# A three-block network on one core: the state-space stage re-paced and its products halved by columns, wider products after two norms

## The chip, the cores and the metric

The kernel runs on one core of a Trainium2 chip. The metric is the device time of the program in microseconds (us), lower is better; a kernel is run several times and the median counts.

## What is computed

One sequence of 512 tokens of width 2048 goes through three layers, in float32. The first is a state-space (S5) layer:

```python
xn = rmsnorm(h, g_pre)
u, z = jnp.split(xn @ w_in, 2, axis=-1)
y = s5_ssm(u, a_re, a_im, log_dt, b_re, b_im, c_re, c_im, d_skip)
y = jax.nn.gelu(y)
y = y * jax.nn.sigmoid(y @ w_glu + b_glu)
y = y * jax.nn.silu(z)
return h + rmsnorm(y @ w_out, g_post)
```

`s5_ssm` runs a complex recurrence of 64 states over the 512 steps in each of 128 groups of 16 channels, plus `d_skip * u`. The second layer is causal attention with forget gates, whose keys, values and gates come from a projection (`shared_kv`) of the first layer's normed output. The third mixes a windowed attention with an RWKV recurrence, after one wide product `h @ w_in_2`, and ends in a product and a norm.

## The kernel before

Activations lie transposed, 16 pages of 128 channels by 512 tokens. A product of float32 accuracy is made of three matmuls: each operand is split into a rounded part and a rest (`hi`, `lo` of the activations by `split`, L165 ff.; `wh`, `wl` of the weights by `wnext`, L188 ff., ScalarE making the first and VectorE the second), and `gemm` (L214) runs hi*wh, lo*wh, hi*wl over 16 k, 48 matmuls of 128x512 per output tile, in four chunks of weights. Weights come by DMA from ScalarE's queue, three chunks ahead.

The stages are `phase1` (32 tiles of `w_in` with the S5 work between them), `phase2` (the gate: 16 tiles, then `out_norm` with 16 tiles of `w_out`, the norm, the residual sum and the next layer's normed activations), `phase4` (value slabs, then 16 key tiles), `phase5` and `phase6` (attention, `out_norm` again), `phase7` and `phase8` (third layer).

In `phase1` the tiles 0 to 15 of `order1` hold u, the rest z; from the sixth tile on a u tile comes every 1.35 tiles. For each u tile j (8 groups) the S5 work is put into a list of due times by `later`, counted in chunks of weights, and `tick` calls what is due: `s5_pool` (GpSimd builds the tables In and Ox for two half-tiles hb), `s5_mats` (kb, the products that make a Toeplitz block, sent by 8 small DMAs of Kt into toep; tb, transposes of In, copied to InT), `s5_phase` (rotation factors Ec, Es), `s5_x` (xb = InT*U, rotation, scan Gs, rotation back to H) and `s5_y` (yb = toep*U + Ox*H, gelu to q, 8 DMAs to y2d). u goes out to memory and comes back as U, regrouped. The S5 matmuls are plain float32 with 64 moving columns (kb and tb 128); a float32 matmul leaves two records in the trace.

The final order of instructions on each engine is made by a scheduler at build time, from the order of these calls and its own model of durations. Each engine runs its instructions strictly in that order. SyncE's queue issues the S5 DMAs and the loads. The pool `tp` of 8 buffers (`tmp`) is shared by everything that is short-lived.

`out_norm` (L743) sums squares, forms the scale (`rstd`, L277), multiplies it into the 16 pages (VectorE for k < 3, GpSimd for the others, L761 and L763), adds the residual (L766 with a permuted token order after the S5 layer, L769 without after attention) and splits. The next products then take the pages k by k: `phase4` with `slab` (L229; four outputs of 272 columns), `phase7` with `gemm`.

```python
self.later(0, self.s5_pool, 2 * j)
self.later(2, self.s5_pool, 2 * j + 1)
self.later(6, self.s5_mats, 2 * j)
self.later(8, self.s5_mats, 2 * j + 1)
...
self.later(10, self.s5_x, j)
self.later(14, self.s5_y, j)
```

Of the kernel before, what the change touches and what calls it, by code (L numbers as in the profile page):

```python
# [42 lines left out]
def lay(inp):  # L43
# [3 lines left out]
    o["xT"] = np.ascontiguousarray(x.reshape(NCK, T, D).transpose(2, 1, 0).reshape(D, S))  # L47
    o["w1"] = _tiles(a["s5_w_in"][0])
# [91 lines left out]
    dd = np.zeros((16, G, 16), np.float32)  # L140
    for c in range(16):
        dd[c, :, c] = a["s5_d"][0].reshape(G, 16)[:, c]
    o["s5dd"] = np.ascontiguousarray(dd.reshape(16, 32, 64).transpose(1, 0, 2))
# [5 lines left out]
class Kern:  # L149
# [80 lines left out]
    def slab(self, act, outs, W, kc=2):  # L230

        nc = self.nc
        for c in range(KT // kc):
# [229 lines left out]

    def s5_pool(self, hb):
# [19 lines left out]
        self.In[hb] = prod("In", Q, B1, B2, 8, 2)  # L484
        self.Ox[hb] = prod("Ox", PT, C1, C2, 9, 5)
        self.dd[hb] = sp.tile([16, 64], F32, tag="dd", name="dd", bufs=4)
        nc.sync.dma_start(self.dd[hb], self.I["s5dd"][hb])

    def s5_mats(self, hb):

        nc, sp = self.nc, self.sp
        In, Ox = self.In.pop(hb), self.Ox[hb]
        kb = self.bank("kb")
        for g in range(4):
            nc.tensor.matmul(kb[:16, g * 128:(g + 1) * 128], In[:, g, 7, :],
                             Ox[:, g, 0:8, :].rearrange("p k c -> p (k c)"), start=True, stop=True)
        tb = self.bank("tb")
        for g in range(4):
            nc.tensor.transpose(tb[:, g * 128:(g + 1) * 128], In[:, g].rearrange("p s c -> p (s c)"), self.ident)
        Kt = sp.tile([16, 4, 128], F32, tag="Kt", name="Kt", bufs=2)  # L500
        k3 = kb[:16].rearrange("p (g k) -> p g k", k=128)
        nc.scalar.activation(Kt[:, :, 16:], k3[:, :, 16:], AF.Copy)

        nc.vector.tensor_tensor(Kt[:, :, :16], k3[:, :, :16], self.dd.pop(hb).rearrange("p (g c) -> p g c", c=16), ALU.add)
        Tp = self.toep[hb % len(self.toep)]
        for s in range(8):
            nc.sync.dma_start(Tp[s * 16:(s + 1) * 16, :, s * 16:128], Kt[:, :, 0:(8 - s) * 16])
        InT = sp.tile([128, 4, 128], F32, tag="InT", name="InT", bufs=3)
        nc.scalar.activation(InT.rearrange("p g k -> p (g k)"), tb, AF.Copy)
        self.InT[hb] = InT  # L510
# [13 lines left out]
    def s5_phase(self, m):  # L524
# [5 lines left out]
        Cc = sp.tile(shp, F32, tag="Cc", name="Cc", bufs=1)  # L530
        Ss = sp.tile(shp, F32, tag="Ss", name="Ss", bufs=1)
# [21 lines left out]
    def s5_x(self, j):  # L553

        nc, sp, v = self.nc, self.sp, self.nc.vector
        U = self.U[j]
# [6 lines left out]
        X = sp.tile([128, 512], F32, tag="X", name="X", bufs=1)  # L563
# [5 lines left out]
        Gs = sp.tile([128, 512], F32, tag="Gs", name="Gs", bufs=1)  # L569
        v.tensor_tensor_scan(Gs, rt.rearrange("p g k -> p (g k)"), X, 0.0, ALU.mult, ALU.add)  # L570
        H = sp.tile([128, 8, 64], F32, tag="X", name="H", bufs=1)
        Hf = H.rearrange("p g k -> p (g k)")
        v.tensor_tensor(Hf, Gs, Ec, ALU.mult)
        v.tensor_tensor(m[0:64], Gs[64:128], Es[64:128], ALU.mult)
        v.tensor_tensor(m[64:128], Gs[0:64], Es[0:64], ALU.mult)
        v.tensor_add(Hf, Hf, m)  # L576
        self.H[j] = H

    def s5_y(self, j):
# [3 lines left out]
        for g in range(8):  # L583
            hb = 2 * j + g // 4
            nc.tensor.matmul(yb[:, g * 64:(g + 1) * 64], self.toep[hb % len(self.toep)][:, g % 4, :], U[:, g, :],
                             start=True, stop=False)
            nc.tensor.matmul(yb[:, g * 64 + 1:(g + 1) * 64],  # L587
                             self.Ox[hb][:, g % 4, 1:9, :].rearrange("p k c -> p (k c)"),
                             H[:, g, 0:63], start=False, stop=True)

        ys = self.tmp("ys")
        nc.scalar.activation(ys, yb, AF.Copy)
        q = self.tmp("q")
        nc.scalar.activation(q, ys, AF.Square)
        v = nc.vector
        v.scalar_tensor_tensor(q, q, 1 / 0.044715, ys, ALU.add, ALU.mult)
        nc.scalar.activation(q, q, AF.Tanh, scale=0.7978845608028654 * 0.044715)
        v.scalar_tensor_tensor(q, q, 1.0, ys, ALU.add, ALU.mult)
# [5 lines left out]
    def run(self):  # L604
        tc, nc, I = self.tc, self.nc, self.I
        v = nc.vector
        with ExitStack() as ex:
# [26 lines left out]
            self.wplan(I["wv0"], [0], 544)  # L634
            self.wplan(I["wv"], range(7))
# [22 lines left out]
    def phase1(self):  # L658
        tc, nc, I, v = self.tc, self.nc, self.I, self.nc.vector
        with ExitStack() as ex:  # L660
# [13 lines left out]
            self.toep = [self.bp.tile([128, 4, 128], F32, name=f"toep{i}") for i in range(4)]  # L674
# [12 lines left out]
            self.sp = None  # L687
            for n in self.order1:
                if n < 16:
                    j = n  # L690
                    if self.sp is None:
                        while self.todo:
                            self.tick()
                        b0.__exit__(None, None, None)
                        self.sp = P(name="sp", bufs=2)
                    self.later(0, self.s5_pool, 2 * j)
                    self.later(2, self.s5_pool, 2 * j + 1)
                    self.later(6, self.s5_mats, 2 * j)
                    self.later(8, self.s5_mats, 2 * j + 1)
# [980 lines left out]
```

## Time and profile before

| | |
|---|---|
| median of 3 runs (lowest, highest) | 3218.8 us (3217.1, 3230.14) |
| the profiled execution | 3217.31 us, span 3215.2 us |
| mean granted TensorE clock | 0.966 of full |
| busy: PE, VectorE, ScalarE, GpSimd | 95%, 58%, 35%, 23% of the span |
| S5 stage, from 118 to 566 us | PE busy 424.41 of 448 us, clock 0.93 |

The span runs from the first to the last instruction of the profiled execution, and 2.1 us of its time lie outside. PE is TensorE. The granted clock is given as a share of full speed, so 0.50 is 1.2 GHz and 1.00 is 2.4 GHz. Matmuls are pipelined: one of 128x512 lasts 0.39 us in the trace, but the next starts 0.23 us after it at full clock, so the distance between starts is what it costs.

### The profile page before, as it was taken

What the parts mean: (1) busy time and instruction counts of PE and PEld (TensorE: products, weight loads), DVE (VectorE), ACT (ScalarE), POOL (GpSimd) and SP (SyncE); (2) the same over time, 40 slices, a digit from 0 to 9 for tenths busy, and PEclk for the clock granted to TensorE, in tenths of its full rate; (3) what the DMA queues carried; (4) which work ended last, traced back from release to release, by engine and by line L of the source; (5) the groups of instructions that cost most, each with busy time, mean ns of one, the idle gap of its engine ahead of it and who ended that gap; (6) DMA issues with size and microseconds to landing.
All of it is one profiled execution on the core that took longest, in us unless ns stands there. A gap on an engine that the chain in (4) does not pass through costs nothing. (4 is left out here: it accounts for less than half of the span.)

```text
span 3215.2 us, 44670 instructions
## 1 busy us (share of the span) xinstructions
PE 3046.9 (95%) x16228; PEld 2511.4 (78%) x16228; DVE 1874.8 (58%) x3171; ACT 1129.8 (35%) x2046; POOL 735.9 (23%) x693
## 2 busy tenths in 40 slices
PE   8899999899989999999999997999889999999897
PEld 6777878688869988888888885777679788777685
DVE  9777676443348333555555337488599566645733
ACT  5243343433323222433333334233222344533322
POOL 0656564110020000000000002233378321122200
PEclk9899999899989999999999998999999999999898
DMA  5344444543343333433333336345742433398533
GB/s 155 109 104 108 110 110 111 186 140 111 95 139 122 109 95 95 125 85 86 89 88 84 92 96 185 108 141 174 180 126 93 122 99 99 108 253 216 159 118 108
DMA packets 347837, 396.29 MB, mean 123 GB/s; under 512 B 138416, under 2 KB 184752, under 8 KB 347616
## 3 DMA queue, kind: packets, MB, share of 16 engines
q10 hardware_dynamic: 131328, 237.43, 26.5%
q1 hardware_dynamic: 216288, 156.00, 16.5%
q8 instruction: 128, 2.10, 0.3%
q14 instruction: 93, 0.76, 0.1%
HBM read 324.59 MB, written 59.80 MB: 120 GB/s over the span
## 5 line engine op out<-in xcount | busy, mean ns | idle before, releaser
L225 PE MATMUL acc<-hi,wh 128*128 128x512 f32 x3232 | 1290.7, 400 | 33.5 <-ACT hi L173 14.6
L226 PE MATMUL acc<-lo,wh 128*128 128x512 f32 x3232 | 1287.2, 399 | 14.6 <-DVE lo L177 11.6
L227 PE MATMUL acc<-hi,wl 128*128 128x512 f32 x3232 | 1287.6, 399 | 10.8 <-DVE wl L199 10.6
L199 DVE TENSOR_TENSOR wl<-raw,wh 128x512 fp32r<-128x512 f32 (+1 forms) x912 | 690.9, 760 | 870.4 <-ACT wh L198 850.2
L198 ACT ACTIVATE wh<-raw 128x512 fp32r<-128x512 f32 (+1 forms) x912 | 571.8, 629 | 1428.3 <-PE acc L226 938.4
L225 PEld LDWEIGHTS acc<-hi,wh 128*128 128x128 f32 x3232 | 617.1, 191 | 176.1 <-ACT hi L173 16.1
L226 PEld LDWEIGHTS acc<-lo,wh 128*128 128x128 f32 x3232 | 616.7, 191 | 164.0 <-DVE lo L177 18.9
L227 PEld LDWEIGHTS acc<-hi,wl 128*128 128x128 f32 x3232 | 616.0, 191 | 152.7 <-DVE wl L199 15.4
L244 PE MATMUL vb<-wh,hi 128*128 128x256 f32 (+2 forms) x768 | 218.8, 288 | 7.6 <-ACT hi L176 5.0
L246 PE MATMUL vb<-wh,lo 128*128 128x256 f32 (+2 forms) x768 | 213.5, 288 | 9.3 <-DVE lo L177 9.2
L245 PE MATMUL vb<-wl,hi 128*128 128x256 f32 (+2 forms) x768 | 219.7, 288 | 1.1 <-DVE wl L199 1.0
L857 POOL TENSOR_TENSOR bm<-bias,cmask 128x512 f32<-128x512 f32 x16 | 21.2, 1326 | 691.5 <-DMA bias<-cumd 458.4
L244 PEld LDWEIGHTS vb<-wh,hi 128*128 128x128 f32 x768 | 147.9, 193 | 8.8 <-ACT hi L176 5.2
L246 PEld LDWEIGHTS vb<-wh,lo 128*128 128x128 f32 x768 | 144.5, 192 | 11.6 <-DVE lo L177 11.3
L245 PEld LDWEIGHTS vb<-wl,hi 128*128 128x128 f32 x768 | 148.2, 193 | 2.8 <-DVE wl L199 2.2
L763 POOL TENSOR_TENSOR y<-y,rstd 128x512 f32<-128x512 f32 x26 | 43.8, 1723 | 411.2 <-ACT rstd L295 411.2
L479 POOL TENSOR_TENSOR In<-Q,bc 128x512 f32<-128x512 f32 x32 | 45.7, 1428 | 251.8 <-DMA bc<-in_s5bc 246.4
L1124 POOL TENSOR_TENSOR wg<-Yi 128x3 f32<-128x3 f32 (+56 forms) x114 | 62.6, 549 | 22.1 <-DVE Yi L1125 14.4
L1125 POOL TENSOR_TENSOR Yi<-Yi,wg 128x3 f32<-128x3 f32 (+56 forms) x114 | 62.7, 550 | 8.6
L587 PE MATMUL yb<-H,Ox 128*128 128x63 f32 x256 | 54.6, 299 | 8.4 <-DVE H L576 8.4
L737 POOL TENSOR_TENSOR ld<-ld 128x512 f32<-128x512 f32 x16 | 20.9, 1308 | 179.2 <-DMA ld<-zd 178.5
L1125 DVE TENSOR_TENSOR Yi<-Yi,w 128x504 f32<-128x504 f32 (+29 forms) x99 | 57.5, 604 | 7.5 <-POOL Yi L1125 7.0
(433 smaller groups left out, 3395.6 us busy)
## 6 DMA issues: line engine op xcount, KB each, us to landing
raw<-in_w ACTq DMA_DIRECT2D x744, 256.0 KB
raw<-in_wk ACTq DMA_DIRECT2D x64, 256.0 KB
raw<-in_wv ACTq DMA_DIRECT2D x56, 256.0 KB
ld<-hd SPq DMA_DIRECT2D x48, 256.0 KB
ld<-y2d SPq DMA_DIRECT2D x32, 256.0 KB
hd<-h SPq DMA_DIRECT2D x32, 256.0 KB
Xd<-X SPq DMA_DIRECT2D x32, 256.0 KB
raw<-in_wd ACTq DMA_DIRECT2D x24, 256.0 KB
```

What stands on the lines that cost most here:

```text
L198: nc.scalar.activation(wh, raw, AF.Copy)
L199: nc.vector.tensor_sub(wl, raw, wh.bitcast(F32))
L225: nc.tensor.matmul(acc, wh[:, sl], hi, start=(kk == 0), stop=False)
L226: nc.tensor.matmul(acc, wh[:, sl], lo, start=False, stop=False)
L227: nc.tensor.matmul(acc, wl[:, sl], hi, start=False, stop=(kk == KT - 1))
L244: nc.tensor.matmul(outs[t], hi[:, tk], wh[:, sl], **st)
L245: nc.tensor.matmul(outs[t], hi[:, tk], wl[:, sl], start=False, stop=False)
L246: nc.tensor.matmul(outs[t], lo[:, tk], wh[:, sl], start=False, stop=(kk == KT - 1 and (W > 256 or t % 2 == 1)))
L479: e.tensor_tensor(o, tr, X1.unsqueeze(2).broadcast_to(shp), ALU.mult)
L587: nc.tensor.matmul(yb[:, g * 64 + 1:(g + 1) * 64], self.Ox[hb][:, g % 4, 1:9, :].rearrange("p k c -> p (k c)"), H[:, g, 0:63], start=False ...
L1124: e.tensor_tensor(w, Y[:, a:a + k, t:t + 1].broadcast_to(shp), Y[:, t:t + 1, t + 1:].broadcast_to(shp), ALU.mult)
L1125: e.tensor_tensor(Y[:, a:a + k, t + 1:], Y[:, a:a + k, t + 1:], w, ALU.add)
```

## The change

The S5 calls are no longer tied to the u tiles: they are all entered at the fifth tile, evenly spaced by 1.35 tiles, with the tables of a tile begun one tile earlier than before. `s5_mats` handles a whole tile at once: kb of four groups goes to four column strips of the array (partitions 0, 32, 64, 96 of one bank), the d_skip diagonal is added by small matmuls with the identity, and eight ScalarE copies take the strips to Kt. xb and yb are computed in column halves (`HALF`), two matmuls of 64 output rows where there was one of 128. gelu reads yb in PSUM, without the copy ys. The second rotation multiplies a copy Gw of the scan with swapped halves, made by ScalarE. X, Gs, Gw, Kt, Cc and Ss come from the shared pool of 8 buffers.

After the S5 layer the permuted write moves from `out_norm` to the gate stage, so that the residual is read from x in natural order (`xn`). In `phase4` the first two value slabs advance together, k pair by k pair, and `phase7` begins with four tiles at once (`gemm4`).

```diff
+    def gemm4(self, act):
+        nc = self.nc
+        accs = [self.pq.tile([128, 512], F32, tag="g", name="acc") for _ in range(4)]
+        ws = []
+        for _ in accs:
+            self.tick()
+            ws.append(self.wnext())
+        for k in range(4):
+            hi, lo = act[k]
+            sl = slice(k * 128, k * 128 + 128)
+            for acc, (wh, wl) in zip(accs, ws):
+                nc.tensor.matmul(acc, wh[:, sl], hi, start=(k == 0), stop=False)
+                nc.tensor.matmul(acc, wh[:, sl], lo, start=False, stop=False)
+                nc.tensor.matmul(acc, wl[:, sl], hi, start=False, stop=False)
+        for c in range(1, 4):
+            for acc in accs:
+                self.gemm(act, acc, [c])
+        return accs
...
+    HALF = slice(0, 64), slice(64, 128)
...
+        for o in range(2):
+            for g in range(4):
+                nc.tensor.matmul(kb[32 * g:32 * g + 16, o * 128:o * 128 + 128], Ins[o][:, g, 7, :],
+                                 self.Ox[2 * j + o][:, g, 0:8, :].rearrange("p k c -> p (k c)"), start=True, stop=False)
+            for g in range(4):
+                c = (4 * o + g) * 16
+                nc.tensor.matmul(kb[32 * g:32 * g + 16, o * 128:o * 128 + 16], self.ident[:, 0:16], dd[:, c:c + 16],
+                                 start=False, stop=True)
...
+            Kt = self.tmp("Kt", (16, 4, 128))
+            for g in range(4):
+                nc.scalar.activation(Kt[:, g, :], kb[32 * g:32 * g + 16, o * 128:o * 128 + 128], AF.Copy)
...
-            nc.tensor.matmul(xb[:, g * 64:(g + 1) * 64], self.InT[2 * j + g // 4][:, g % 4, :], U[:, g, :],
-                             start=True, stop=True)
+            for hs in self.HALF:
+                nc.tensor.matmul(xb[hs, g * 64:(g + 1) * 64], InT[g // 4][:, g % 4, hs], U[:, g, :],
+                                 start=True, stop=True)
...
+        Gw = self.tmp("Gw")
+        nc.scalar.activation(Gw[0:64], Gs[64:128], AF.Copy)
+        nc.scalar.activation(Gw[64:128], Gs[0:64], AF.Copy)
         v.tensor_tensor(Hf, Gs, Ec, ALU.mult)
-        v.tensor_tensor(m[0:64], Gs[64:128], Es[64:128], ALU.mult)
-        v.tensor_tensor(m[64:128], Gs[0:64], Es[0:64], ALU.mult)
-        v.tensor_add(Hf, Hf, m)
+        v.tensor_tensor(m, Gw, Es, ALU.mult)
+        v.tensor_sub(Hf, Hf, m)
...
-        ys = self.tmp("ys")
-        nc.scalar.activation(ys, yb, AF.Copy)
...
-        v.scalar_tensor_tensor(q, q, 1.0, ys, ALU.add, ALU.mult)
+        v.scalar_tensor_tensor(q, q, 1.0, yb, ALU.add, ALU.mult)
...
+            for i, n in enumerate(self.order1):
+                if i == ZF - 1:
...
+                    for j in range(16):
+                        for f, dt, a in ((self.s5_pool, 0, 2 * j), (self.s5_pool, 2 * UR, 2 * j + 1),
+                                         (self.s5_mats, 9, j), (self.s5_phase, 9, j // 2),
+                                         (self.s5_x, 14, j), (self.s5_y, 19, j)):
+                            if f != self.s5_phase or j % 2 == 0:
+                                self.later(int(4 * UR * j + dt), f, a)
...
+            v.scalar_tensor_tensor(m.rearrange("p (k s) -> p s k", s=T), w(t), 1.0, w(y2), ALU.add, ALU.mult)
...
+            if s == 1:
+                for c in range(8):
+                    self.slab(self.hk, o0, 272, part=[c])
+                    self.slab(self.hk, outs, 256, part=[c])
...
+                if n == 0:
+                    held = self.gemm4(x7)
+                acc = self.gemm(x7) if n > 3 else held[n]
```

Where the instructions move: first TensorE in the middle of the S5 stage. acc is a tile of the wide product, the other names are those of the S5 steps above. Before:

```order
L225 MATMUL acc<-hi,wh 128x512
L495 MATMUL kb<-Ox,In 16x128 x4
L499 MATMUL tb<-ident,In 128x128 x2
L559 MATMUL xb<-U,InT 128x64 x4
L499 MATMUL tb<-ident,In 128x128 x2
L226 MATMUL acc<-lo,wh 128x512
```

In the changed program, the burst in its place:

```order
L228 MATMUL acc<-hi,wl 128x512
L592 MATMUL xb<-U,InT 64x64 x16
L522 MATMUL kb<-Ox,In 16x128 x4
L527 MATMUL kb<-dd,ident 16x16 x4
L522 MATMUL kb<-Ox,In 16x128 x4
L527 MATMUL kb<-dd,ident 16x16 x4
L540 MATMUL tb<-ident,In 128x128 x8
L621 MATMUL yb<-U,toep_302 64x64 x2
L226 MATMUL acc<-hi,wh 128x512
```

What stood as two or three pieces per tile is one burst. The remaining 30 yb matmuls of the tile, which need H, follow its xb after 21 to 26 matmuls of acc in nine of the 16 tiles (31 to 67 in the others), where before it was 36 to 60 in all but the first. From one xb to the next stand between 19 and 150 matmuls of acc.

SyncE's queue where the S5 stage hands over to the gate stage: zd takes the z tiles, y2d the S5 outputs q, and y2d is read back as ld. Before:

```order
L713 DMA zd_126<-z 128x512
L722 DMA ld<-y2d_97 128x512
L601 DMA y2d_112<-q 16x8x64 x8
L713 DMA zd_127<-z 128x512
L713 DMA zd_128<-z 128x512
L722 DMA ld<-y2d_98 128x512
```

In the changed program:

```order
L745 DMA zd_126<-z 128x512
L636 DMA y2d_112<-q 16x8x64 x8
L745 DMA zd_127<-z 128x512
L745 DMA zd_128<-z 128x512
L754 DMA ld<-y2d_97 128x512
L754 DMA ld<-y2d_98 128x512
```

The last S5 outputs leave before the last z tiles, and all loads stand behind the last zd. On TensorE the last yb now has 26 matmuls of acc behind it in the stage, where before it had none.

TensorE after the second norm (hi and lo are the normed pages, the four acc are the first four tiles). Before:

```order
L292 MATMUL rsb<-ident,rc 128x128 x4
L225 MATMUL acc<-hi,wh 128x512
L226 MATMUL acc<-lo,wh 128x512
L227 MATMUL acc<-hi,wl 128x512
L225 MATMUL acc<-hi,wh 128x512
```

In the changed program:

```order
L313 MATMUL rsb<-ident,rc 128x128 x4
L243 MATMUL acc<-hi,wh 128x512 x4
L244 MATMUL acc<-lo,wh 128x512
L245 MATMUL acc<-hi,wl 128x512
L244 MATMUL acc<-lo,wh 128x512
L245 MATMUL acc<-hi,wl 128x512
L244 MATMUL acc<-lo,wh 128x512
L245 MATMUL acc<-hi,wl 128x512
L244 MATMUL acc<-lo,wh 128x512
L245 MATMUL acc<-hi,wl 128x512
L243 MATMUL acc<-hi,wh 128x512 x4
```

Each page k now feeds twelve matmuls where it fed three, and four of them need only hi.

## Rows read from the trace of the kernel before

**Rows 1.** Stretches: us, busy (count) of PE PEld DVE ACT POOL, PEclk, DMA, GB/s.

```profile
486.00:494.00 8.00, 8.00 (x38) 7.52 (x37) 3.75 (x7) 3.39 (x6) 7.35 (x7) 0.57 0.35 104
118.00:566.00 448.00, 424.41 (x2280) 353.82 (x2280) 313.47 (x370) 165.77 (x281) 267.80 (x185) 0.93 0.42 107
...
2836.00:2916.00 80.00, 74.34 (x906) 58.95 (x905) 45.28 (x60) 30.10 (x55) 20.67 (x17) 1.00 0.95 246
```

**Rows 2.** Groups by line, TensorE, 118 to 566 us: a third of the wide product.

```profile
L225 PE MATMUL acc<-hi,wh 128*128 128x512 f32 x376 | 153.4, 408 | 0.0
```

**Rows 3.** Timeline, TensorE: start us, us, engine, line, out<-in; around two S5 bursts.

```profile
245.13 0.39 PE L226 MATMUL acc<-lo,wh 128*128 128x512 f32 x1
...
247.15 0.39 PE L225 MATMUL acc<-hi,wh 128*128 128x512 f32 x1
...
253.59 0.40 PE L226 MATMUL acc<-lo,wh 128*128 128x512 f32 x1
...
260.98 0.39 PE L225 MATMUL acc<-hi,wh 128*128 128x512 f32 x1
```

**Rows 4.** Timeline, TensorE, third layer: matmuls that write half or a quarter of the rows.

```profile
2162.50 1.09 PE L1081 MATMUL xg<-AR,BK 64*64 64x128 f32 x28
...
2967.34 0.40 PE L225 MATMUL acc<-hi,wh 128*128 128x512 f32 x1
2967.67 0.27 PE L1239 MATMUL yb<-XI,UV 128*64 128x64 f32 x1
...
2970.01 0.39 PE L227 MATMUL acc<-hi,wl 128*128 128x512 f32 x1
```

**Rows 5.** TensorE's waits, 118 to 566 us: total, times, longest.

```profile
PE kb L495 <- POOL Ox L481: 15.1, 10, 5.3
PE yb L587 <- DVE H L576: 8.4, 4, 3.9
```

**Rows 6.** Timeline, VectorE: first and last step between xb and H, tiles 0 and 15.

```profile
135.99 0.69 DVE L565 TENSOR_TENSOR X<-xb,Ec 128x512 f32<-128x512 f32 x1 [0.45 <-PE xb L559]
148.29 1.70 DVE L576 TENSOR_TENSOR H<-H,mX 128x512 f32<-128x512 f32 x1
...
551.24 0.69 DVE L565 TENSOR_TENSOR X<-xb,Ec 128x512 f32<-128x512 f32 x1 [2.05 <-PE xb L559]
559.14 0.69 DVE L576 TENSOR_TENSOR H<-H,mX 128x512 f32<-128x512 f32 x1
```

**Rows 7.** SyncE's queue: two DMA lines (ns min/median/max), and its longest wait.

```profile
L507 SPq DMA_DIRECT2D toep<-Kt x256: 559/593/1581, 125.2 to 554.1; - x128
L521 SPq DMA_DIRECT2D U<-ud x128: 303/430/1766, 103.1 to 537.3; - x128
SPq L507 <- DMA raw<-in_w: 34.1, 17, 4.6
```

**Rows 8.** Timelines at the hand-over to the gate stage: TensorE, and SyncE's queue.

```profile
579.10 0.80 PE L225 MATMUL acc<-hi,wh 128*128 128x512 f32 x1 [3.85 <-ACT hi L173]
...
585.69 0.42 PE L227 MATMUL acc<-hi,wl 128*128 128x512 f32 x1
575.41 11.11 SPq L722 DMA_DIRECT2D ld<-y2d  x16
```

**Rows 9.** After two norms: us, PE busy (matmuls), PEclk, DMA, GB/s; first with lo.

```profile
938.20:990.00 51.80, 33.51 (x201) 0.74 0.51 163
1948.50:2000.00 51.50, 31.49 (x106) 0.70 0.55 171
955.73 1.27 PE L246 MATMUL vb<-wh,lo 128*128 128x272 f32 x4 [5.54 <-DVE lo L177]
1965.15 0.80 PE L226 MATMUL acc<-lo,wh 128*128 128x512 f32 x1 [6.82 <-DVE lo L177]
```

**Rows 10.** VectorE's residual sum with the permuted order and without (ns min/median/max).

```profile
L766 DVE SCALAR_TENSOR_TENSOR h<-y,cols,ld x16: 1170/1482/2187, 944.7 to 981.0; 128x512 f32<-128x512 f32 x16
L769 DVE SCALAR_TENSOR_TENSOR h<-y,cols,ld x16: 740/1020/1762, 1955.4 to 1986.2; 128x512 f32<-128x512 f32 x16
```

More of the change, by code (lines that the diff above doesn't have):

```diff
@@ L228, in gemm, with slab @@
         return acc
-    def slab(self, act, outs, W, kc=2):
+    def gemm4(self, act):
         nc = self.nc
-        for c in range(KT // kc):
+        accs = [self.pq.tile([128, 512], F32, tag="g", name="acc") for _ in range(4)]
[14 more added lines that the diff above has]
+        return accs
+    def slab(self, act, outs, W, kc=2, part=None):
+        nc = self.nc
+        for c in range(KT // kc) if part is None else part:
             if c * kc % 2 == 0:
@@ L491, in s5_mats @@
+    def s5_mats(self, j):
         nc, sp = self.nc, self.sp
-        In, Ox = self.In.pop(hb), self.Ox[hb]
+        Ins = [self.In.pop(2 * j + o) for o in range(2)]
         kb = self.bank("kb")
[L494 to L508, printed above, removed]
@@ new lines, in s5_mats @@
+        InT = self.InT[j] = []
+        Tp = self.toep[j % len(self.toep)]
+        for o in range(2):
+            Kt = self.tmp("Kt", (16, 4, 128))
+            for g in range(4):
+                nc.scalar.activation(Kt[:, g, :], kb[32 * g:32 * g + 16, o * 128:o * 128 + 128], AF.Copy)
+            for s in range(8):
+                nc.sync.dma_start(Tp[s * 16:(s + 1) * 16, 4 * o:4 * o + 4, s * 16:128], Kt[:, :, 0:(8 - s) * 16])
+        for o in range(2):
+            tb = self.bank("tb")
+            for g in range(4):
+                nc.tensor.transpose(tb[:, g * 128:(g + 1) * 128], Ins[o][:, g].rearrange("p s c -> p (s c)"), self.ident)
+            InT.append(sp.tile([128, 4, 128], F32, tag="InT", name="InT", bufs=3))
+            nc.scalar.activation(InT[o].rearrange("p g k -> p (g k)"), tb, AF.Copy)
@@ L673, in phase1 @@
             r = self.rstd(ss, 1e-6)
-            self.toep = [self.bp.tile([128, 4, 128], F32, name=f"toep{i}") for i in range(4)]
+            self.toep = [self.bp.tile([128, 8, 128], F32, name=f"toep{i}") for i in range(2)]
             for t in self.toep:
@@ L792, in phase4 @@
                 nc.tensor.matmul(x, self.zero, self.hk[0][0], start=True, stop=False)
-            self.slab(self.hk, [b[t // 2][:, t % 2, :] for t in range(4)], 256)
+            outs = [b[t // 2][:, t % 2, :] for t in range(4)]
+            if s == 1:
+                for c in range(8):
+                    self.slab(self.hk, o0, 272, part=[c])
+                    self.slab(self.hk, outs, 256, part=[c])
+            else:
+                self.slab(self.hk, outs, 256)
             rc = self.rc
```

100 lines of the change are left out of this document (42 added, 58 removed).

## The prediction

> **What bounds the kernel now.** I read the page's table of engines first: TensorE is busy 95% of the span, and its row in 40 slices dips at three kinds of places: the stretch of the S5 stage, the hand-over behind it, and the two norms. Everywhere else nothing of this change can be gained, since PE is already full there. So the sum is made of what TensorE loses at those places.
>
> In the S5 stage, 118 to 566 us, PE is busy 424.4 of 448 us at a mean clock of 0.93 [rows 1]. What fills it: the wide product has 3 x 376 = 1128 matmuls there [rows 2], each 0.2285 us from start to start at full clock, 257.7 us. The S5 matmuls are read from the timeline as the distance between two wide matmuls around a burst, less the wide matmuls themselves. 245.13 to 247.15 with 8 records of kb and 4 of tb between: 2.02 - 0.46 = 1.56 us. 253.59 to 260.98 with the same and 32 records of yb and 16 of xb: 7.39 - 0.46 = 6.93 us [rows 3]. The 48 records of yb and xb thus cost 5.37 us, 0.112 each. A tile j takes 5.37 + 2 x 1.56 = 8.49 us, 16 tiles 136 us. One minus the mean clock, times 448 us, is 31 us lost at 1.2 GHz; they lie in seven stretches of 4 to 15 us, the last from 486 to 494 [rows 1], and each begins in a burst of S5 matmuls or in a pause of PE. Some 28 of the 31 fell on a busy PE. 257.7 + 136 + 28 = 422, against 424.4 measured: the stage is understood. The remaining 23.6 us are waits, 15.1 of kb for GpSimd's Ox and 8.4 of yb for H [rows 5].
>
> **The sum, made against the profiled execution's 3217.3 us** (span 3215.2 and 2.1 outside; the median of the three runs lies 1.5 above it).
>
> *a. Column halves, -40 us.* The third layer already has the form: yb of half rows, 64 columns moving. From 2967.34 to 2970.01 stand three wide matmuls and 62 such records [rows 4]: 2.67 - 0.46 = 2.21 us; within the run they start 0.029 us apart, 62 x 0.029 = 1.80, so 0.41 is left for going in and out. Two halves cost 0.058 where a whole costs 0.112. Per tile: 96 half records x 0.0295 = 2.83. The 16 main records of kb now go to four strips; the nearest row is xg, quarters with 128 moving columns, 28 records in 1.09 us less the last one's 0.27, 0.030 each [rows 4], so 0.5 us; if the strips did not overlap they would cost 1.9 as now. The 16 small records of the diagonal have no row: between 0 and a half record's 0.029 each, I take the upper end, 0.5. tb stays, about 1.0. Three bursts in and out of the divided array, by the 0.41 of the row: 1.2. Sum 6.0 against 8.49, 2.5 us x 16 = 40. Bounds: 17 with kb at its present cost, 59 if going in and out cost nothing.
>
> The Trainium skill, page TensorEngine Tiling (Array Packing), section Tiling Modes, says that a change of tiling mode drains the array, which speaks against many short bursts. The row agrees, with its 0.41 us; without the drain this term would be 59 and not 40, and the row decides.
>
> *b. Clock, -14 us.* Bursts of halves run densely: in the third layer from 2836 to 2916, with several of them, the clock is 1.00 throughout [rows 1]. That would give back all 28. But kb and tb stay, and so do pauses at yb (next term), after which the clock also fell. I take half. Bounds 0 and -28.
>
> *c. Waits, -4 us.* Tables begun a tile earlier take GpSimd's 15.1 away [rows 5]. What comes late next is H. From X to the end of H VectorE needs 12.3 + 1.7 = 14.0 us, 8.6 in the last tile, and over the 16 pairs on average 10.8 [rows 6]. One multiplication of H's chain goes, and the swap by ScalarE comes in, beside the multiplication by Ec; I count these as even. In nine tiles the order leaves between xb and the yb that needs H only 21 to 26 wide matmuls, 5 to 6 us, and the rest of the burst, 3 us: 8 to 9 us. That lacks about 2 us, 18 in nine tiles; with 2 for other waits 20 us stand against 23.6. While PE waits at yb, wide matmuls that are ready are queued behind it. Bounds: 8 and 38 us of waits, -15 and +14.
>
> The other edits of the stage cost nothing by themselves. VectorE is busy 313 of 448 us and loses work (the two additions into Kt, one of H's four steps); ScalarE is busy 166 us with 281 instructions [rows 1], 0.59 each, and gets seven more per tile (eight copies of strips and two swapped halves in place of two copies and ys): at that price 66 us, and there is room. If VectorE's cover goes, H comes later still, which is a rival. X, Gs, Gw, Kt, Cc and Ss from the shared pool make X wait for the DMAs that read a Kt; SyncE sends 16 of these per tile either way.
>
> *d. Hand-over, -5 us.* Now the last yb ends at 566.3, PE restarts in earnest at 579.10 and runs at half speed until 585.69 [rows 8]: 19.4 us, in which 4 us of work at full clock get done, 15 lost. In the changed order 26 wide matmuls (5.9 us) follow the last yb, so the S5 chain is covered; but all loads stand behind the last z. I put the last z, three steps of 0.69 [rows 6] and their hand-overs, at 2.5 us after PE's end and its own DMA's issue at 0.3; from SyncE's first of the 16 issues at 575.41 to PE's start at 579.10 are 3.7 us [rows 8], load and split together: a pause of 6.5, then the same 6.6 us at half speed, 10 lost. The 16 loads are issued 0.69 us apart [rows 8] before and after. Bounds 0 and -10.
>
> *e. First norm, -9 us.* From 938.2 to 990 PE does 201 slab matmuls [rows 9]; by their 272 columns against 512 one is 0.121 us at full clock, 24.4 in all, so 27.4 are lost. The residual sum without permutation takes 0.74 to 1.76 us in place of 1.17 to 2.19 [rows 10], 0.43 less; five of them stand ahead of the first lo on VectorE, which comes 2.1 us earlier than 955.73 [rows 9]. From then a page feeds 24 matmuls, 2.8 us at full clock, about what VectorE needs for the page's two steps beside GpSimd; PE stays busy and the clock returns after the 6.6 us seen at the hand-over. Lost: 15.4 of pause less 1.9 of work on hi, 3.3 at half speed, 1.5 of gaps: 18.3. The permutation, now in the gate stage, adds 0.43 us to a VectorE step there that PE does not wait for. Bounds -4 and -12.
>
> *f. Second norm, -5 us.* 106 wide matmuls from 1948.5 to 2000 [rows 9] are 24.2 us, 27.3 lost. The first lo stays at 1965.15 [rows 9]. Twelve matmuls per page, four on hi alone: pause 16.7 - 0.9, half speed 3.3, gaps 2. A new wait of about 2 us: four tiles finish together and hold all four banks, so the fifth waits for the first to be emptied. 23 against 27.3. Bounds -2 and -7.
>
> -40 - 14 - 4 - 5 - 9 - 5 = -77: **3140 us.**
>
> **The rivals.**
>
> *H paces the stage.* If VectorE, beside a busier GpSimd, keeps the mean of 10.8 us [rows 6] and the nine tiles lack 3 us each, 28 of waits, and the pauses keep the clock as it is: +10 + 14, 3164. For it: H already makes PE wait with twice the distance [rows 5]; against it: the chain's shortest are near 8. Chance 0.17.
>
> *SyncE's queue paces it.* Per tile 16 DMAs of toep at 0.593, 16 of U and y2d at 0.43 [rows 7], and about four others make 18.6 us of issuing; its waits in the stage, 27 rows of which the longest total is 34.1, sum to 108.5, 6.8 per tile. If these stay, 25.4 x 16 = 406 us, where my stage has 390: +16, and the clock +14: 3170. Against it: many of these waits are slack. Chance 0.12.
>
> *The pacing does not come about.* The scheduler writes the order, and in it from 19 to 150 wide matmuls stand between one xb and the next. Clock and waits stay as they are, b and c nothing: 3158. Chance 0.08.
>
> *Small records cannot start 0.029 us apart here.* Were the spacing 0.062, yb and xb would take 5.95 per tile, 3.1 more: 3190. Chance 0.03. The Trainium skill, page TensorE: Matmul & The Clock Gate, Part 1, gives about 62 ns per matmul as the sequencer's bound with hardware decode off; the row of the third layer speaks against it.
>
> *Slower: the halves do not overlap.* Both halves share one moving operand U, which in the third layer they do not. If each half costs the 0.112 us of a whole, yb and xb take 10.8 per tile: with the rest 13.9, 5.4 more than now, a = +87: 3267. With b to f at -37 the change loses from 0.08 us per half record on. Against it: 0.029 measured [rows 4]. Chance 0.05.
>
> **How the numbers follow.** The forecast has 0.55; it is 3140. Range 3096 to 3185: the lower end has b, e and f at their good bounds, a, c and d well on the way to theirs (-51 - 28 - 15 - 8 - 12 - 7 = -121), the upper end takes in the first three rivals; left out are the last two, 0.08, the tops of the first two, 0.05, and the forecast's own tails, 0.06. 0.5% is what a measurement of this kernel can tell from no change, 16 us. Faster holds all but the slower rival (0.05) and the top of the H and spacing rivals (0.04): 0.91, 0.04, 0.05.
>
> **What would show it.** Right: from first kb to last yb some 390 us with 1128 wide matmuls; yb and xb about 2.8 us a tile, starts 0.03 apart; kb no longer waiting for GpSimd, yb for H some 18 us; half clock in 3 or 4 stretches; the first slab and first tiles of layer three dense from the first lo on. Wrong: half records 0.06 or more apart; SyncE without a gap through the stage; the clock at half as often as before; or PE waiting for weights, behind a ScalarE or VectorE held by a DMA.

## The result, and the profile after

The changed kernel takes 3261.24 us (median of 4 runs, 3258.59 to 3263.05) against 3221.93 for the kernel before beside it (3217.1 to 3230.14): a ratio of 1.0119, 95% interval 1.0095 to 1.0143. It is slower by 1.2%, where the forecast had 3140 and gave the slower side 0.05. The profiled run has 3258.59, a span of 3256.8 and a mean clock of 0.959.

**Where the time went.** Three instants that both programs have, read from TensorE's timeline: the end of the last yb, the first matmul of the statistics (ssb, the sum of squares) at either norm, and what is left of the span behind the second.

| us | last yb ends | ssb, norm 1 | from there to ssb, norm 2 | rest of the span |
|---|---|---|---|---|
| before | 566.3 | 935.3 | 1010.5 | 1269.4 |
| after | 607.6 | 979.9 | 1006.2 | 1270.7 |

All of the loss lies in the S5 stage: it ends some 41 us later, with 26 wide matmuls still to do where there were none. The stretches of the stage (columns as in [rows 1]: busy us of PE, PEld, VectorE, ScalarE, GpSimd, then PE's clock, the DMA share, GB/s):

```profile
120.00:160.00 40.00, 36.10 (x281) 28.68 (x282) 31.22 (x28) 20.13 (x43) 37.02 (x25) 1.00 0.37 97
...
240.00:280.00 40.00, 24.48 (x250) 19.82 (x246) 30.19 (x27) 15.55 (x30) 26.29 (x17) 0.78 0.31 73
...
480.00:520.00 40.00, 22.09 (x189) 18.45 (x190) 22.73 (x26) 14.45 (x28) 11.14 (x8) 0.71 0.35 91
...
560.00:600.00 40.00, 26.30 (x207) 21.36 (x203) 20.75 (x31) 14.94 (x31) 0.00 (x0) 0.82 0.40 94
```

No engine is full in the later ones. From 100 to 640 us TensorE idles 127.1 us (before: 38.7). One minus the clock, summed over stretches of 20 us, comes to 68.8 us (before: 39.2), but much of that fell on an idle TensorE; on a busy one 39.7 us were lost (before: 32.8). What is left of its busy time, less the wide matmuls at 0.2285 us, is the S5 work at full clock: 87.1 us (before: 139.5). The account closes: 52 us of work less, 88 of idle time and 7 of clock more make 43, and 188 wide matmuls fewer are done by 640 us (1252, before 1440), 43 us. TensorE's waits in that window of the changed kernel (us in total, times, longest):

```profile
PE acc L226 <- DVE u L547: 42.7, 8, 9.4
PE xb L592 <- DMA y2d<-q: 36.3, 7, 9.8
PE acc L226 <- ACT hi L174: 8.8, 1, 8.8
PE xb L592 <- DMA raw<-in_w: 8.4, 2, 6.5
PE acc L226 <- DVE z L741: 7.4, 2, 5.4
PE yb L624 <- DVE H L611: 6.2, 2, 4.5
PE xb L592 <- DMA U<-ud: 4.6, 3, 2.7
PE kb L522 <- POOL Ox L505: 3.3, 3, 1.8
```

The two waits of [rows 5] have shrunk, 15.1 to 3.3 for GpSimd's Ox and 8.4 to 6.2 for H. Two that were not there have come: for a PSUM bank that VectorE has not emptied into u, and ahead of xb, 49 us by three names. What the engines do around one such pair, from the timeline of the changed kernel (start, duration, engine, line, operation, tiles, count, idle time before and what ended it):

```profile
244.01 2.02 DVE L603 TENSOR_TENSOR_SCAN Gs<-rt,X 128x512 f32<-128x512 f32 x1
246.06 1.53 DVE L609 TENSOR_TENSOR H<-Gs,Ec 128x512 f32<-128x512 f32 x1
247.51 1.70 DVE L565 TENSOR_TENSOR Cc<-e,e 128x512 f32<-128x512 f32 x1
249.14 1.59 DVE L568 TENSOR_TENSOR Ss<-e,e 128x512 f32<-128x512 f32 x1
250.65 0.68 DVE L547 TENSOR_TENSOR u<-acc,rstd 128x512 f32<-128x512 f32 x1
...
251.47 0.77 PE L226 MATMUL acc<-hi,wh 128*128 128x512 f32 x1 [7.09 <-DVE u L547]
...
248.49 10.21 SPq L536 DMA_DIRECT2D toep<-Kt  x16
258.80 0.53 SPq L549 DMA_DIRECT2D ud<-u  x1
259.43 2.62 SPq L493 DMA_DIRECT2D bc<-in_s5bc  x2
262.14 7.57 SPq L553 DMA_DIRECT2D U<-ud  x8
269.81 5.20 SPq L636 DMA_DIRECT2D y2d<-q  x8
...
272.64 1.97 PE L592 MATMUL xb<-U,InT 128*64 128x64 f32 x32 [6.46 <-DMA raw<-in_w]
...
274.65 0.69 DVE L598 TENSOR_TENSOR X<-xb,Ec 128x512 f32<-128x512 f32 x1 [4.81 <-PE xb L592]
```

Read it as a loop. VectorE takes u out of its bank only behind the scan, the tables Cc and Ss and a step of H, so TensorE stands still for 7.09 us. u is there at 251.33, but SyncE is in the middle of its 16 issues of toep, and the gaps between them, until 258.70; ud goes out at 258.80, the loads of U at 262.14 to 269.71, and xb starts at 272.64, after a pause of 6.46. The releaser named is another DMA; by the program the one that had to land was U's. X, the scan and H of this tile then come later by as much, and the next u stands behind them. The xb burst ran at half clock (32 records in 1.97 us; 1.15 at full clock, below). The order that the scheduler wrote says the same without a time: in ten of the sixteen tiles xb stands exactly 196 wide matmuls behind the last of its u, four tiles and four matmuls, that is, u is taken out only when all four banks are full; in the kernel before it stands 90 to 175 behind, 130 on average.

### The profile page after: what moved, and what is told of

Read it like the earlier page. It is cut to its first block, busy times and chain, and to the rows that moved or that the text cites. A ratio compares the mean times of both kernels' runs of the same rounds, so it can differ in the third digit from the quotient of the medians.

```text
span 3256.8 us, 46728 instructions
## 1 busy us (share of the span) xinstructions
PE 3005.0 (92%) x17252; PEld 2465.5 (76%) x17252; DVE 1878.6 (58%) x3123; ACT 1154.4 (35%) x2158; POOL 742.3 (23%) x691
## 4 chain that ended last, share of the span: by engine, by line
PE 69%; DVE 12%; DMA 6%; POOL 5%; issue 3%; SPq 3%; ACT 2%; ACTq 0%; DVEq 0%; POOLq 0%
PE acc L226 19%; PE acc L227 19%; PE acc L228 18%; DVE wl L200 2%; PE vb L266 2%; PE vb L267 2%; PE vb L265 2%; DMA raw<-in_w 1%; POOL wg L1163 1%; POOL Yi L1164 1%; PE ob L948 1%; PE pt L931 1%; DVE h L799 1%; DVE w L1163 1%; SPq L553 1%
## 5 line engine op out<-in xcount | busy, mean ns | idle before, releaser
L226 PE MATMUL acc<-hi,wh 128*128 128x512 f32 x3216 | 1291.0, 402 | 84.4 <-DVE u L547 42.7
L200 DVE TENSOR_TENSOR wl<-raw,wh 128x512 fp32r<-128x512 f32 (+2 forms) x912 | 682.6, 751 | 913.6 <-ACT wh L199 881.9
L199 ACT ACTIVATE wh<-raw 128x512 fp32r<-128x512 f32 (+2 forms) x912 | 569.8, 627 | 1418.0 <-PE acc L227 931.1
L228 PEld LDWEIGHTS acc<-hi,wl 128*128 128x128 f32 x3216 | 614.2, 191 | 157.5 <-DVE wl L200 15.1
L592 PE MATMUL xb<-U,InT 128*64 128x64 f32 x512 | 23.8, 260 | 50.6 <-DMA y2d<-q 36.3
L592 PEld LDWEIGHTS xb<-U,InT 128*64 128x64 f32 x512 | 21.6, 171 | 55.9 <-issue 37.9
```

The costliest lines, as they stand in the source:

```text
L199: nc.scalar.activation(wh, raw, AF.Copy)
L200: nc.vector.tensor_sub(wl, raw, wh.bitcast(F32))
L226: nc.tensor.matmul(acc, wh[:, sl], hi, start=(kk == 0), stop=False)
L228: nc.tensor.matmul(acc, wl[:, sl], hi, start=False, stop=(kk == KT - 1))
L592: nc.tensor.matmul(xb[hs, g * 64:(g + 1) * 64], InT[g // 4][:, g % 4, hs], U[:, g, :], start=True, stop=True)
```

## The experiments

Theories: **1**, SyncE's in-order queue paces the stage, U's loads stand behind 16 issues of toep. **2**, the shared pool of eight buffers: Kt, held until its DMAs have read it, and X, Gs, Gw, Cc, Ss now take buffers that u, z and q need. **3**, x follows u too closely, since x is paced evenly and u is not. Ratios are to the kernel before on the same chip (95% intervals). Sums of 303 to 393 us of issuing in the expectations add up the rows of SyncE's timeline with the gaps inside a row, single ones of them up to 8 us long; record by record the issues are 317 us in the kernel before, 304 after, 224 in toep8t.

**toep_act**: toep issued by ScalarE.
```
-                nc.sync.dma_start(Tp[s * 16:...], Kt[...])
+                nc.scalar.dma_start(Tp[s * 16:...], Kt[...])
```


> The changed kernel, with the 16 DMAs that write a tile's toep issued from ScalarE's queue in place of SyncE's; nothing else. Theory 1 (SyncE's in-order queue paces the stage: the loads of U stand behind 16 issues of toep): the waits of TensorE for U and for u, some 90 us, mostly go, and the time falls from 3261 by 50 us or more, to 3210 or less. Theory 2 (the shared pool of eight buffers: u, X, Cc and Ss wait for a buffer that a DMA still reads): Kt is read by the same DMAs, a little earlier; a gain of 5 to 20 us. Theory 3 (x follows u too closely since only x is paced evenly): u is no earlier, below 15 us either way.


Measured: 3255.18, ratio 1.0102 (1.0080 to 1.0124). Theory 1 missed in this form. The waits for u are gone from the head of the list, and others stand there: ScalarE, which also splits the weights, is now late with them.
```profile
PE acc L228 <- DVE wl L200: 21.8, 11, 3.6
PE acc L226 <- ACT wh L199: 18.1, 10, 3.5
PE yb L624 <- DVE H L611: 17.1, 5, 4.9
```
The Trainium skill (Trainium Kernel Development and Optimization, Key Constraints) says that issuing from several engines only saves the sequencer's issue time. Here it was moved and not saved: SyncE issues for 141 us of the stage in place of 304, ScalarE for 162 us more, and the time falls by 6 us.

**kt_own**: Kt out of the shared pool.
```
-            Kt = self.tmp("Kt", (16, 4, 128))
+            Kt = sp.tile([16, 4, 128], F32, tag="Kt", name="Kt", bufs=2)
-        self.Ox[hb] = prod("Ox", PT, C1, C2, 9, 8)
+        self.Ox[hb] = prod("Ox", PT, C1, C2, 9, 6)
```


> The changed kernel, with Kt in two buffers of its own instead of the shared pool; to make room, Ox has six buffers in place of eight. Theory 1 (SyncE's queue): within 8 us of 3261. Theory 2 (shared pool): the two buffers that are held longest leave the pool of eight, u is taken out of its bank earlier, and the time falls by 20 us or more, to 3240 or less. Theory 3 (x too close behind u): within 8 us.


Measured: 3220.59, 0.9996 (0.9983 to 1.0008): 41 us of the changed kernel's time, as theory 2 had it, though by another wait than it named: u's stays, and the waits ahead of xb fall from 49 us to 20. SyncE's queue, in which U's loads stand, is held less: from 118 us to the end of the stage it waits 15.6 us for Kt in the changed kernel and 10.7 here, and for u, first the changed kernel, then kt_own:
```profile
SPq L549 <- DVE u L547: 33.5, 6, 6.8
...
SPq L549 <- DVE u L547: 10.5, 4, 5.6
```
TensorE's waits in kt_own:
```profile
PE acc L226 <- DVE u L547: 42.9, 8, 8.1
PE xb L592 <- DMA U<-ud: 14.3, 4, 7.9
...
PE xb L592 <- DMA y2d<-q: 5.7, 3, 3.1
```

**tied**: due times counted from u.
```
-  ((self.s5_pool, 0, 2 * j), (self.s5_pool, 2 * UR, 2 * j + 1), (self.s5_mats, 9, j), ...
+  ((self.s5_pool, 0, 2 * j), (self.s5_pool, 2 * UR, 2 * j + 1)):
...
+  if n < 16:
+      self.later(6, self.s5_mats, j); self.later(10, self.s5_x, j); self.later(15, self.s5_y, j)
```


> The changed kernel, with the products of a tile (tables to TensorE, x, y) due again at fixed distances behind the begin of that tile's u, 6, 10 and 15 steps, while GpSimd's tables stay a tile ahead and evenly paced. Theory 3 (x too close behind u: 2.5 to 6.5 steps in place of 6.5): the waits for U go, and the time falls by 40 us or more, to 3220 or less. Theory 1 (SyncE's queue) and theory 2 (shared pool): the same DMAs and the same buffers are asked for, within 15 us of 3261.


Measured: 3230.23, 1.0029 (1.0018 to 1.0041), 31 us below the changed kernel: less than theory 3 asked for, more than the others allowed. In a few tiles (j = 3 is the first) the toep of tile j + 2 is written before the yb of j reads it, so that part of y comes from the wrong tables; the instructions are the same. The wait for u is 1.4 us here, and yb waits 53.8 us for toep, which now stands behind U. One queue, and whatever comes second in it is late. As a test of theory 3 it is inconclusive.

**before_pool**: the kernel before with X, Gs, Cc, Ss and Kt in the shared pool (H, which shared X's buffer, gets its own).
```
-        Kt = sp.tile([16, 4, 128], F32, tag="Kt", name="Kt", bufs=2)
+        Kt = self.tmp("Kt", (16, 4, 128))
...
```


> The kernel before, with X, Gs, Cc, Ss and the two Kt moved to the shared pool of eight buffers, as the change does, and nothing else. Theory 2 (shared pool): this alone makes it slower by 15 us or more, 3237 or above. Theories 1 and 3: within 8 us of 3222.


Measured: 3242.68, 1.0064 (1.0044 to 1.0083), +22 us, the last yb ends at 585.8 in place of 566.3. Theory 2 stands in both directions. Its new wait is TensorE's bank again, held behind a VectorE that is itself held:
```profile
PE yb L587 <- DVE H L576: 13.0, 4, 8.2
...
PE acc L225 <- DVE Kt L504: 10.7, 3, 4.8
```

**u_own, ku_own**: u in two buffers of its own; with and without Kt.
```
-        u = self.tmp("u")
+        u = sp.tile([128, 512], F32, tag="u", name="u", bufs=2)
```


> The changed kernel, with u in two buffers of its own instead of the shared pool, and Ox with six buffers in place of eight. Theory 2 (shared pool), form a: it is u's own wait for a pool buffer that keeps TensorE's banks full; its 43 us of waits for u go, and with them part of the waits for U: 3215 or less. Form b: it is the two Kt buffers, held for 16 DMAs, that make the pool short, and X, Cc and Ss would wait on as they do; within 10 us of 3261. Theory 1 (SyncE's queue): within 10 us of 3261.

> The changed kernel, with Kt and u in two buffers of their own each; for the room, Ox has five buffers in place of eight and In three in place of four. Theory 2 (shared pool): the waits for u that were left with Kt alone out of the pool (42.9 us) mostly go, and the time falls below 3195. Theory 1 (SyncE's queue, 369 us of issuing in the stage) as the next limit: the stage can't come under some 400 us, and the time stays at 3205 to 3222. GpSimd may show: with five Ox its tables have less lead, 5 to 10 us of waits at kb.


Measured: 3219.54, 0.9995 (0.9984 to 1.0007), and 3214.10, 0.9973 (0.9961 to 0.9985). u alone gives as much as Kt alone (its waits fall to 13.8 us; nearest to form a, which had 3215 or less), both together only 6 us more; there u still has 20.4 us of waits, 17.2 of them in one. So the pool explains why the change lost, and something else keeps the gain away; that is where ku_own's reading by theory 1 holds. The pool seems to act less through waits for a buffer in the run than through the order that the scheduler wrote for it: from 118 us to the end of the stage VectorE's idle time that a DMA ended is 14.6 us in the changed kernel, 10.0 in the kernel before. No run separates the two.

**halves, norm1**: one part of the change at a time, on the kernel before.
```
-            nc.tensor.matmul(xb[:, g * 64:(g + 1) * 64], self.InT[2 * j + g // 4][:, g % 4, :], U[:, g, :], ...
+            for hs in (slice(0, 64), slice(64, 128)):
+                nc.tensor.matmul(xb[hs, g * 64:(g + 1) * 64], self.InT[2 * j + g // 4][:, g % 4, hs], U[:, g, :], ...
```


> The kernel before, with only the x and y products of the S5 tiles in column halves; pacing, pools, tables, gelu and norms as before. In the changed kernel these products take 1.08 and 1.98 us per tile at full clock, where they took 5.37: 2.3 us less, 37 in 16 tiles. If TensorE paces the stage in the kernel before: 3185, and 5 to 10 lower where the clock holds better. If SyncE's queue (387 us of issues in the 448 us) or H paces it as soon as TensorE has less to do: half of it or less is seen, 3200 to 3222, and the waits for H or U grow by what is missing.


Measured: 3218.44, 0.9989 (0.9974 to 1.0005). The estimate of 37 us less work was high; counted as for the changed kernel, S5 work fell by 26 us (139.5 to 114.0). Of these 3.5 are seen in the median. TensorE's idle time from 100 to 640 us rose from 38.7 to 66.1 us, by these waits among others:
```profile
PE xb L560 <- ACT InT L509: 21.8, 7, 5.7
PE kb L495 <- POOL Ox L481: 19.8, 9, 5.2
PE yb L590 <- DVE H L577: 10.9, 3, 5.4
```
In [rows 5] GpSimd's Ox had 15.1 and H 8.4; InT, ScalarE's copy of tb, had 4.3. None of the three is a DMA. norm1 (the hunks of the gate stage, the residual's layout and the slabs, from the diff as they stand):


> The kernel before, with only the first norm's part of the change: the permutation at the gate stage, the residual read from the other layout, the first two slabs in alternation. By the lag of the changed kernel, 44.65 us at the first norm's statistics and 40.32 at the second's, it gains 4.3 us: 3217 to 3218. By the forecast it gains 9: 3213. If what the changed kernel gained there was an accident of its later start: 3222.


Measured: 3209.53, 0.9964 (0.9952 to 0.9977), 12 us, more than any of its three readings had, of which the interval between the two statistics shows 5.5. In the profiled run the S5 stage also ends 3.5 us earlier and the part behind the second statistics is 4.2 us shorter; the edit touches neither, so those are not shown to be its doing.

**toep8t, toep8, toep8_n1**: one Kt per tile, 8 DMAs of eight groups.
```
+        Kt = sp.tile([16, 8, 128], F32, tag="Kt", name="Kt", bufs=1)
...
+        for s in range(8):
+            nc.sync.dma_start(Tp[s * 16:(s + 1) * 16, :, s * 16:128], Kt[:, :, 0:(8 - s) * 16])
```


> The changed kernel, with one Kt per tile in a buffer of its own (16x8x128) and its toep written by 8 DMAs of eight groups in place of 16 of four; Ox has six buffers in place of eight. It takes as much room as the run kt_own, which has two buffers of half the size and 16 DMAs. Theory 1 (SyncE's in-order queue is the stage's next limit): 8 issues of 0.6 to 0.75 us less per tile, some 80 us of issuing in the stage; against kt_own's 3220.6 it falls by 20 us or more, to 3200 or less. Theory 2 alone (pool): no buffer of the pool is freed that kt_own does not free, 3213 to 3228. If TensorE's waits for H limit it (21 us in ku_own): 3205 to 3215.

> As toep8t, and u in two buffers of its own; Ox has five buffers, In three. Same room as ku_own (3214.1). Theory 1: against ku_own 25 us or more, to 3189 or less, with SyncE's issue time in the stage at some 300 us in place of 392. Theory 2 alone: within 8 us of 3214. The forecast's own sum had 3140: that far only if neither H nor a bank is waited for.

> As toep8, without the change at the second norm (four tiles of the third layer side by side on the first pages). In the changed kernel the lag against the kernel before grows by 2.0 us across the second norm, where 5 were to be gained. If that is the side-by-side tiles' doing (they ask for four weight tiles at once): 2 us below toep8, and TensorE's waits for weights near the first tiles of the third layer go. If the forecast's mechanism holds there: 5 us above toep8. Both are near what a comparison can tell; the times at which the statistics of the norm and the first products behind it start are read for it.


Measured: 3175.88, 0.9867 (0.9852 to 0.9882); 3184.05, 0.9888 (0.9873 to 0.9903); 3183.21, 0.9884 (0.9867 to 0.9900). Half as many DMAs for toep, in the same room, are worth 45 us by the medians of kt_own and toep8t, 42 by their ratios: theory 1 in its second form, the largest single effect found. That it is their issuing, not their transfer, is argued: the DMA engines are busy 0.43 of kt_own's stage, 0.47 of toep8t's. u's own buffers are worth nothing any more, and GpSimd's shorter lead may cost some. The second norm's part shows no difference (0.8 us; from ssb to the first kq, the first tile that ScalarE takes out of layer three's products, 84.4 and 84.5).

**toep8t_full**: toep8t with full-width products.


> As toep8t (3175.9), with the x and y products back to full width. Column halves were worth 3.5 us in the kernel before (run halves), where SyncE issued DMAs for 393 us of the stage; here it issues for 303. If TensorE paces the stage once SyncE has room, the 2.3 us of a tile come back: 3205 to 3215, and the rest of the gain over the kernel before (some 10 us) is the first norm and the hand-over. If H, GpSimd or the remaining queue paces it: below 3190, and the halves are worth little here too.


Measured: 3173.02, 0.9856 (0.9838 to 0.9874), the fastest version found, 1.4% below the kernel before and 2.6% below the changed one by their ratios. Column halves are worth next to nothing here either: the last yb ends at 523.1 with them and at 525.8 without, and the medians have it the other way round. TensorE's S5 work is 30 us less with them (90.2 against 120.0), and it idles 23 us more (57.9 against 35.2). Its waits, first toep8t, then toep8t_full:
```profile
PE yb L624 <- DVE H L611: 16.5, 5, 4.3
...
PE xb L592 <- issue: 4.3, 1, 4.3
...
PE xb L592 <- DMA toep<-Kt: 3.7, 2, 2.3
PE xb L592 <- DMA zd<-z: 3.6, 1, 3.6
```
```profile
PE tb L540 <- DVE q L630: 14.1, 4, 6.8
PE yb L621 <- DVE H L610: 9.9, 7, 3.9
...
PE xb L591 <- DMA U<-ud: 1.1, 1, 1.1
```

**f_gel, f_noswap, h_gel_noswap**: gelu from a copy in SBUF; scan halves swapped by VectorE; both, with halves.
```
+        ys = self.tmp("ys")
+        nc.scalar.activation(ys, yb, AF.Copy)
...
-        Gw = self.tmp("Gw")
-        nc.scalar.activation(Gw[0:64], Gs[64:128], AF.Copy)
-        nc.scalar.activation(Gw[64:128], Gs[0:64], AF.Copy)
...
```


> As toep8t_full (3173.0), with the gelu again from a copy of yb in SBUF instead of from the bank. In toep8t_full TensorE waited 14.1 us at tb for VectorE's last gelu step, which frees the bank. If the bank held longer is a limit of the stage: that wait goes and 5 to 14 us are gained, 3159 to 3168. If it is slack that the next wait (H, 9.9 us) takes up, or ScalarE's extra copy costs as much: 3170 to 3178.

> As toep8t_full (3173.0), with the scan's halves swapped by VectorE's two half multiplications again, without ScalarE's copies. From the end of the scan to the end of H the chain took 4.5 us on average in the kernel before, 5.8 in the changed one and 6.1 in toep8t_full. If H paces the stage: 1.2 to 1.6 us per tile, the wait for H (9.9 us) falls to some 3 us, 3160 to 3168. If VectorE's additional step takes it back or the stage is paced elsewhere: 3170 to 3178.

> As toep8t (3175.9, column halves), with both of the edits of the two other runs: gelu from SBUF, scan halves swapped by VectorE. If H and the bank that gelu holds are what kept the halves' 37 us from being seen: well below both others, 3140 to 3158. If the halves are worth little whatever is done there: within 8 us of the better of the two others.


Measured: 3209.14, 0.9949 (0.9932 to 0.9967); 3194.23, 0.9901 (0.9877 to 0.9926); 3195.87, 0.9915 (0.9891 to 0.9938). Both edits, undone, cost where a gain was thought possible: by the ratios 30 and 14 us, and in all three the last yb ends at 545 to 547, some 20 us later than in toep8t_full. So gelu from PSUM and the swap by ScalarE are good parts of the change, with the queue relieved. The wait at tb for gelu did go in f_gel, and the time rose all the same: a wait that ends last is not yet a price. From X to the end of H VectorE took 11.5 us on average in toep8t_full, 12.4, 13.9 and 14.9 in these three; but f_gel also adds a holder to the pool, and the account says that waits, H's among them, are not what cost the time: from 100 to 640 us TensorE idles 39.8 us in f_gel and 36.9 in f_noswap against 35.2, while half clock on a busy TensorE took 35.1 and 39.4 us against 18.0. In these two nearly all that was lost came as clock, and why the clock was lower there is open.

## Why the prediction was wrong, by its steps

Two steps failed. That the pool and its DMAs cost nothing (c) turned the change into a loss: taking Kt out of the pool gave back 41 us. That work taken off TensorE is time of the stage (a) kept the gain away.

**What bounds the kernel.** "The stage is understood" rested on TensorE being busy 424.4 of 448 us [rows 1]. Taking work away from TensorE alone gave 3.5 us of 26 (halves), and at most 3 of 30 with the queue relieved (toep8t against toep8t_full); in the changed kernel with Kt out of the pool, 8 DMAs less per tile gave 45. A busy share of 95% said that TensorE had little slack, not that nothing else had as little. SyncE's queue had little more: in the kernel before it issued for 317 of the 448 us, and 89 us more went into 50 gaps of over 0.3 us between issues. That SyncE held the kernel before as well is argued: no run relieved its queue there, and the waits that grew in halves name ScalarE's InT, GpSimd's Ox and H. The Trainium skill (Perfetto Trace Analysis, Optimization Strategy) reads consistent bubbles on the engine that should be full as a possible sign of too few buffers for the next tile; kt_own and before_pool agree, with -41 and +22 us.

**a, column halves, -40.** That halves overlap was right, and the size was too small. Tiles at full clock in the changed kernel:
```profile
451.43 1.15 PE L592 MATMUL xb<-U,InT 128*64 128x64 f32 x32 [1.79 <-DMA y2d<-q]
452.51 0.41 PE L522 MATMUL kb<-Ox,In 128*16 128x128 f32 x8
...
453.16 1.09 PE L540 MATMUL tb<-ident,In 128*128 128x128 f32 x8
...
464.03 0.33 PE L624 MATMUL yb<-H,Ox 128*64 128x63 f32 x4 [1.71 <-DVE H L611]
...
465.93 0.23 PE L527 MATMUL kb<-dd,ident 128*16 128x16 f32 x8
...
605.35 0.39 PE L226 MATMUL acc<-hi,wh 128*128 128x512 f32 x1
605.67 0.33 PE L624 MATMUL yb<-H,Ox 128*64 128x63 f32 x4
...
607.57 0.50 PE L227 MATMUL acc<-lo,wh 128*128 128x512 f32 x1
```
xb takes 1.08 us, kb 0.65 with its diagonals where the forecast had 1.0. Half records start 0.03 apart, also with a common moving operand, so the rivals of the spacing and of halves that do not overlap are out. Going in and out cost less than the 0.41 of the forecast: the 60 records of yb take 1.99 us between wide matmuls (605.35 to 607.57, less one), 0.2 over their spacing. Taken that way a tile is 5.0 us, 2.67 for xb, kb and tb in one burst and 0.36 and 1.99 for yb, where 8.49 stood: 55 us in 16 tiles, and the account above has 52. But the term was taken as time of the stage, and alone it is worth some 3 us there.

**b, clock, -14.** It came out at +7: the forecast counted, rightly, only what half clock takes from a busy TensorE, and that went from 32.8 to 39.7 us. The forecast's own reason, pauses, fits: each of the 17 falls to half clock from 118 to 640 us in the changed kernel comes behind a pause. But idle time alone does not give the loss: toep8t idles 57.9 us and loses 21.2 to the clock, the kernel before 38.7 and 32.8.

**c, waits, -4, and the edits that "cost nothing".** Idle grew by 88 us. Ox behaved as forecast, and H, put at some 18 us, took 6.2. What failed is one sentence: that the shared pool makes X wait for DMAs that read a Kt, but that "SyncE sends 16 of these per tile either way". It priced a longer hold of a buffer by the number of DMAs, and named neither u, which needs the same buffers to free TensorE's bank, nor U's loads, which stand behind toep in the queue. With -52 of a and +7 of b this makes 43; the lag at the first statistics is 44.7. That the swap is even, and the gelu from PSUM free, was wrong too, to the good side: undone they cost 14 and 30 us with the queue relieved.

**d, hand-over, -5.** TensorE restarts at 622.64 and is at full clock at 626.45, 18.9 us behind the last yb with 34 wide matmuls (7.8 us) done: 11.1 lost in place of 15 [rows 8]. -4 is right.

**e, first norm, -9.** From one norm's statistics to the other's the changed kernel takes 4.4 us less. Over all kernels run, the 14 with this part take 1002.3 to 1009.4 us, the three without 1010.5 to 1012.6: 6.6 us between the means. The first lo came 1.1 us earlier behind the statistics than before, not 2.1: the five h ahead of it took 8.02 us beside GpSimd where they took 9.47, 0.29 less apiece and not the 0.43 of the medians [rows 10]. First the kernel before, then the changed one:
```profile
944.67 9.47 DVE L766 SCALAR_TENSOR_TENSOR h<-y,cols,ld 128x512 f32<-128x512 f32 x5
...
989.57 8.02 DVE L799 SCALAR_TENSOR_TENSOR h<-y,cols,ld 128x512 f32<-128x512 f32 x5
...
997.52 1.75 DVE L178 SCALAR_TENSOR_TENSOR lo<-h,cols,hi 128x512 fp32r<-128x512 f32 x1
```

**f, second norm, -5.** Nothing, or a small loss: from ssb to the first kq 86.0 us against 83.9 before, 84.4 with the part and 84.5 without in toep8 and toep8_n1. The fuller start came and was paid back. Counted from ssb, the 50th wide matmul starts 6.0 us earlier with the part (35.7 in toep8, 41.7 in toep8_n1), the 100th at the same time (53.2 and 53.3). The forecast priced a wait of 2 us for a bank; what came were waits for the weights of the tiles that follow, the longest of 2.69 us at 2022.01 in the changed kernel. Its own figures, 23 against 27.3, give -4 and not -5.
```profile
2006.07 0.79 PE L244 MATMUL acc<-lo,wh 128*128 128x512 f32 x1 [5.56 <-DVE lo L178]
...
2022.01 0.50 PE L226 MATMUL acc<-hi,wh 128*128 128x512 f32 x1 [2.69 <-ACT wh L199]
```

**The rivals.** "SyncE's queue paces it" had the right engine, but its 25.4 us per tile was no bound that any run kept: X follows X by 27.7 us on average in the kernel before, 30.6 after, and that toep8t and toep8t_full come to 25.3 is chance, since their queue issues for 14 us per tile. It took the queue's waits as fixed; the gaps over 0.3 us between SyncE's issues grew from 89 to 147 us of the stage. So the sign given for it, SyncE without a gap, did not come, though the queue mattered. "H paces the stage" (its 28 us of waits against 20 make +8 and not +10) named one thing that is left: with the queue relieved H is TensorE's first or second wait. No slower rival spoke of the pool.

What stays open: what paces the stage at some 25 us per tile in toep8t and toep8t_full alike. H, the loads of U and banks held by VectorE each have a part of TensorE's waits, and no run separates them. How the pool acts, by its buffers or by the order that the scheduler writes around them, stays open too. That six Ox in place of eight do nothing by themselves was not tried either.

## What to carry to other kernels

Before you take work off the busiest engine, price every in-order queue of the stage per tile as well, its issues and the waits that hold what is queued behind; where one has as little room, the saving turns into waiting, and fewer DMAs (here 8 of eight groups in place of 16 of four) can be worth more than the arithmetic saved. Add up work, idle time and clock separately, since a change can save the first and pay in the others. When tiles move to a shared pool, list for each how long it is held and by what, a DMA above all, and who needs the next buffer to free a PSUM bank. Judge a part of a change by instants that both programs share, close around it.

## What was not expected of the hardware

Two things. Two halves of a product overlap although they share the moving operand, and so do four strips of 16 columns: 32 records of kb and its diagonals take 0.65 us. And the code behind the second norm's statistics, the same in twelve of these kernels, took between 1268.4 us (ku_own) and 1280.0 (toep8t) in the profiled runs: a part worth under some 10 us can't be judged by the total of one run.
